# A diffusion backbone's last stretch, turned from features x tokens to tokens x features

## The chip, the cores and the metric

The kernel runs on one core of a Trainium2 chip. A core has TensorE for matmuls (the profile lists its weight loads apart, as PEld), VectorE (DVE), ScalarE (ACT), GpSimd (POOL) and SyncE (SP), which here issues nearly all DMAs. The metric is the time of one execution on the device in microseconds (us), less is better. Times are medians of several runs; the profile is of one execution, taken by the hardware profiler.

## The reference

Two layers work on 256 latent tokens and 256 context tokens of 1024 features. Layer 0 mixes tokens with a convolution module, layer 1 with a bidirectional mLSTM of 4 heads; each is followed by an MLP with a squared ReLU. Shift, scale and gate of every sub-layer (`sh1, sc1, g1, sh2, sc2, g2`) come from a map of a conditioning vector, called adaLN; the latents use `c`, the context `c_ctx`. Only the latents are returned, so in layer 1 the context ends with the mixer's state.

```python
def adaln(cvec, w, b):
    return jnp.split(jax.nn.silu(cvec) @ w + b, 6, axis=-1)

def mlstm_output(feats, h_f, h_b, gn_g, skip, w_down):
    ...
    y = (hn.astype(xc.dtype) + skip * xc) * jax.nn.silu(z)
    return y @ w_down

...
        u = modulate(h, sh1, sc1)
...
        h = layer_norm(ALPHA * h + g1 * y, ln1_g[i], ln1_b[i])
        h = layer_norm(ALPHA * h + g2 * sq_relu_mlp(modulate(h, sh2, sc2), mlp_w1[i], mlp_w2[i]), ln2_g[i], ln2_b[i])
```

## The kernel before

All activations stand as features x tokens: 128 features on the partitions, tokens along the free axis. A matmul therefore takes a 128x128 block of a weight as its stationary operand and lets the tokens move past it: 512 columns where latents and context go together, 256 where only the latents are left, which is the case in the queries, the output gates, `w_down` and the whole last MLP.

Every product is made of three matmuls (`mm3`, lines 175 to 181): the operands are split into a rounded high part and the remainder, and high x high, high x low and low x high are summed in PSUM. Weights arrive by `raw_load` (1 MB, three buffers, line 150) on SP's queue; `split` (lines 154 and 155) makes the high part on ScalarE and the low part on VectorE, four buffers of 128x1024 each, `wh` and `wl`.

The adaLN map is cut into 12 units of 512 outputs for each layer. `Ada` computes a unit on TensorE (line 291). `AdaV` computes it on VectorE: a step loads 128x512 of the weight into the one buffer `ar` (line 353) and adds its product with a scalar column to an accumulator, once for each of the two streams, context and latents (lines 357 and 359). After eight steps, `rows` sums over the partitions with a matmul by ones (line 372), and `end` transposes the result to feature columns. Layer 1's units 0 to 3 run so during layer 0's MLP (`ada_n1`), units 4 to 8 during the mLSTM's projections (`ada_n2`): one step for each half group of the value projection's last 16, for every second one of the queries, and for every second key tile. The last three units, 9 to 11, run on TensorE after the last down projection, as `fill` between the parts of a norm.

Of layer 1's mixer the diff touches the end. `pair` builds the scores of two heads: 16 key tiles, each projected (272 columns) and multiplied with the conv output (512 columns). Then `Z.att` lists what runs beside what: `o` output gates, `W` decay weights, `A` attention with group norm, `D` the down projection of a head; the number is how many steps of the side chain go with one step of the main one. `down(h)` has eight output tiles, each of 12 matmuls, and line 1417 adds gate times product to the residual `hl`.

A layer norm over features on the partitions is `Norm`: `feed` adds up tiles as they come, takes a mean by a matmul after four (line 446), shifts and squares (lines 461, 466 and 467); `finish` sums by matmuls with a column of ones (line 474), computes the statistics, and spreads them over all partitions with one more matmul (line 507); `apply` multiplies and adds (lines 513 and 514). After the last head `finish` runs with the `fill` units between its parts; the affine then makes the MLP's input `u2` (lines 1459 to 1461).

The last MLP runs in four parts of 1024 hidden features. Each part makes its hidden tiles (w1, eight output tiles, relu, square, split) and multiplies them with w2: eight output tiles of 24 matmuls, each added to `hl` by line 924. The norm is fed in part 3; then line 1475 applies gain and bias and line 1476 stores features x tokens. The host transposes the result.

A scheduler orders each engine's instructions: it takes those that are ready by its own model of the times, in program order where several are. An engine works its queue strictly in order. `pin` keeps chosen matmuls in program order.

## Time and profile before

| | us |
|---|---|
| Median of three runs | 1799.55 |
| Lowest and highest | 1798.92, 1805.72 |
| The profiled execution | 1797.44 |
| Its span, first to last instruction | 1795.7 |

| Engine | busy us | share |
|---|---|---|
| TensorE, matmul | 1743.1 | 97% |
| TensorE, weight load | 1513.9 | 84% |
| VectorE | 1111.0 | 62% |
| ScalarE | 762.7 | 42% |
| GpSimd | 8.4 | 0% |

Busy time of a matmul counts from its start to the modelled end of its pipeline, so neighbours overlap; the pace of TensorE is read from the distance of starts. The granted clock is given for a stretch as a share of full speed. A row of the timeline names start, duration, engine, line, operation, out <- in, the shapes and how many neighbours were merged; in brackets stands how long the engine idled before it and what released it. The stage of the heads ends at about 1567 us, the last MLP runs from 1589.6 to 1778.6 us.

### The profile page before, as it was taken

The page shows a single profiled execution, that of the slowest core. Times are in us where ns is not written, and L with a number is a line of the kernel's source. Part 1 is how long each engine was busy: PE and PEld are TensorE (multiplying, and loading weights), DVE is VectorE, ACT ScalarE, POOL GpSimd, SP SyncE. Part 2 cuts the span into 40 slices and gives each one's busy share as a digit, 9 for nine tenths or more (in the row PEclk, how much of TensorE's full clock was granted, in tenths as well). Part 3 has the DMA queues.
Part 4 walks back from the last instruction along what each step waited for, and adds up shares of the span by engine and source line. Part 5 has one row for each costly group of instructions (what it writes and reads, how often), then busy time and mean ns, then how long its engine had stood idle before and what let it go on. Part 6 is the DMA issues. An engine that isn't in the chain of part 4 may idle for free.

```text
span 1795.7 us, 28106 instructions
## 1 busy us (share of the span) xinstructions
PE 1743.1 (97%) x11410; PEld 1513.9 (84%) x11410; DVE 1111.0 (62%) x2071; ACT 762.7 (42%) x1212; POOL 8.4 (0%) x60
## 2 busy tenths in 40 slices
PE   8999999999999999999999999999999999889996
PEld 5564998878789999966779999988999999869996
DVE  6556996565546878741336644533777767876666
ACT  4311763232223555531424323323767744434443
POOL 0000000000000000000000000000000000000000
PEclk9999999999999999999999999999999999989998
DMA  9424416344323275677546533533534355555551
GB/s 354 157 97 147 158 60 228 123 141 140 112 94 118 82 239 162 206 248 269 211 143 236 205 103 131 185 132 118 186 138 178 120 186 192 173 202 187 186 188 48
DMA packets 67251, 295.65 MB, mean 165 GB/s; under 512 B 6771, under 2 KB 22643, under 8 KB 36145
## 3 DMA queue, kind: packets, MB, share of 16 engines
q1 hardware_dynamic: 49456, 279.16, 44.6%
q10 hardware_dynamic: 17664, 14.69, 2.5%
q8 instruction: 90, 1.47, 0.3%
q14 instruction: 41, 0.33, 0.1%
HBM read 278.09 MB, written 15.73 MB: 164 GB/s over the span
## 4 chain that ended last, share of the span: by engine, by line
PE 88%; DVE 5%; ACT 3%; DMA 2%; issue 1%; SPq 0%; ACTq 0%; DVEq 0%
PE mm L177 25%; PE mm L181 25%; PE mm L180 24%; DVE wl L155 2%; DMA raw<-ada_w 1%; PE fl L291 1%; ACT wh L154 1%; PE fl L718 1%; PE cv L787 1%; PE ln L177 1%; PE ln L181 1%; PE ln L180 1%; PE mm L762 1%; PE cv L181 1%; PE cv L180 1%
## 5 line engine op out<-in xcount | busy, mean ns | idle before, releaser
L154 ACT CAST wh<-raw 128x1024 fp32r<-128x1024 f32 x354 | 367.7, 1048 | 611.2 <-PE mm L180 520.7
L155 DVE TENSOR_TENSOR wl<-raw,wh 128x1024 fp32r<-128x1024 f32 x354 | 430.7, 1221 | 303.4 <-ACT wh L154 301.4
L180 PE MATMUL mm<-u,wh 128*128 128x256 f32 (+1 forms) x1400 | 447.5, 320 | 0.0
L177 PE MATMUL mm<-u,wh 128*128 128x256 f32 (+1 forms) x1272 | 398.5, 314 | 7.4 <-ACT u L1459 2.1
L181 PE MATMUL mm<-u,wl 128*128 128x256 f32 (+1 forms) x1272 | 396.6, 313 | 0.5 <-DVE wl L155 0.5
L180 PEld LDWEIGHTS mm<-u,wh 128*128 128x128 f32 x1400 | 268.3, 192 | 18.5 <-DVE mv L522 0.8
L177 PEld LDWEIGHTS mm<-u,wh 128*128 128x128 f32 x1272 | 243.8, 192 | 29.6 <-ACT wh L154 7.4
L181 PEld LDWEIGHTS mm<-u,wl 128*128 128x128 f32 x1272 | 244.2, 192 | 16.4 <-DVE wl L155 2.3
L177 PE MATMUL mm<-hid,wh 128*128 128x256 f32 (+1 forms) x512 | 166.0, 324 | 0.0
L181 PE MATMUL mm<-hid,wl 128*128 128x256 f32 (+1 forms) x512 | 165.3, 323 | 0.0
L180 PE MATMUL mm<-hid,wh 128*128 128x256 f32 (+1 forms) x512 | 165.3, 323 | 0.0
L177 PE MATMUL mm<-xl,wh 128*128 128x256 f32 x512 | 146.4, 286 | 0.9 <-ACT wh L154 0.7
L180 PE MATMUL mm<-xl,wh 128*128 128x256 f32 x512 | 145.2, 284 | 0.6 <-DVE xl L155 0.6
L181 PE MATMUL mm<-xl,wl 128*128 128x256 f32 x512 | 145.1, 284 | 0.2
L359 DVE SCALAR_TENSOR_TENSOR L<-ar,cs,L 128x512 f32<-128x512 f32 x126 | 90.0, 748 | 56.8 <-DMA ar<-ada_w 56.7
L177 PEld LDWEIGHTS mm<-hid,wh 128*128 128x128 f32 x512 | 97.4, 190 | 7.9 <-issue 0.2
L180 PEld LDWEIGHTS mm<-hid,wh 128*128 128x128 f32 x512 | 97.5, 190 | 7.7 <-issue 0.2
L181 PEld LDWEIGHTS mm<-hid,wl 128*128 128x128 f32 x512 | 97.4, 190 | 7.5
L177 PE MATMUL mm<-xm,wh 128*128 128x512 f32 x256 | 102.9, 402 | 0.0
L177 PEld LDWEIGHTS mm<-xl,wh 128*128 128x128 f32 x512 | 97.8, 191 | 3.7 <-issue 1.7
L181 PE MATMUL mm<-xm,wl 128*128 128x512 f32 x256 | 100.3, 392 | 0.0
L180 PEld LDWEIGHTS mm<-xl,wh 128*128 128x128 f32 x512 | 97.9, 191 | 1.7 <-DVE xl L155 0.8
(417 smaller groups left out, 3006.0 us busy)
## 6 DMA issues: line engine op xcount, KB each, us to landing
raw<-w SPq DMA_DIRECT2D x64, 1024.0 KB, 4.9
raw<-wo SPq DMA_DIRECT2D x32, 1024.0 KB, 4.8
raw<-ada_w SPq DMA_DIRECT2D x30, 1024.0 KB, 5.0
ar<-ada_w SPq DMA_DIRECT2D x72, 256.0 KB, 2.8
raw<-wv SPq DMA_DIRECT2D x16, 1024.0 KB, 5.4
raw<-wqT SPq DMA_DIRECT2D x16, 1024.0 KB, 5.5
raw<-wq SPq DMA_DIRECT2D x16, 1024.0 KB, 5.3
raw<-wk SPq DMA_DIRECT2D x16, 1024.0 KB, 4.9
```

The source lines that it names most:

```text
L154: c = nc.scalar.copy(hi, src)
L155: nc.vector.tensor_tensor(lo, src, hi.bitcast(F32), op=ALU.subtract)
L177: a = nc.tensor.matmul(ps, wh, xh, start=start, stop=False)
L180: nc.tensor.matmul(ps, wh, xl, start=False, stop=False)
L181: nc.tensor.matmul(ps, wl, xh, start=False, stop=stop)
L291: a = nc.tensor.matmul(ps[32 * j:32 * j + 32], cs[:, kt, 14 - 2 * v:46 - 2 * v], blocks[kt], start=first and kt < 4, stop=last and kt >= 4 ...
L359: nc.vector.scalar_tensor_tensor(a, w, c, a, op0=ALU.mult, op1=ALU.add)
L718: nc.tensor.matmul(wqs[0][32 * j:32 * j + 32, :], wgp[0][:, kt, :], raw[:, j * 512:(j + 1) * 512], start=kt == 0, stop=kt == ET - 1, tile_ ...
L762: nc.tensor.matmul(xfs[b], fm, A[0:fm.shape[0], t, sl], start=i == 0, stop=i == len(w_) - 1)
L787: return nc.tensor.matmul(o[r:r + 64, :], g_[:, r:r + 64], ps_[b][i], start=i == 0, stop=i == 1, tile_position=(0, r))
```

## The change

From `w_down` on, the latents stand as tokens x features: 128 tokens on the partitions, 1024 features along the free axis. The activations become the stationary operand, the weights move, 512 columns at a time.

- The residual is transposed once, when the layer's input is made, into `R` (16 TensorE transposes, ScalarE copies), in place of `hl`.
- `down` does two halves of 512 features x two token tiles, 12 matmuls each. VectorE multiplies by the gate row `G1`, GpSimd adds to `R` (VectorE in the last head). It yields four times for a head instead of eight, and the pace in `Z.att` beside head 3 doubles. The last head's order is token tile by token tile, and its second half of weights is split into `pw` buffers.
- The norms take their statistics along the free axis (`bn_stats`, an iterated reciprocal root, all on VectorE). `ln1` transposes the normed tile back for w1, which stays as it was: weights stationary, 256 tokens moving.
- w2's products accumulate in four PSUM banks over all 32 depth tiles. The last four depth tiles are done for token tile 0 first, so that its `finish` lies beside token tile 1. Gain and bias are rows; the output is stored as tokens x features.
- `fill` is gone. Units 6 to 9 are computed by `AdaV` for the latents alone. Units 4, 5, 10 and 11, the gates, go through the new `AdaR`, which adds the bias to a row and stores it in DRAM; `rows` loads it back to all partitions. `ada_n2` steps at every key tile. Units 0 to 3 stay as they were.
- The eight `sel` copies become broadcast views of the identity. The host lays `wdown` and `w2_1` out anew and passes six rows (`rows_d`).

```diff
-    att = [['o0', 'G0 W0 W1', 2.4], ['o1', 'A0 W2', 2.6], ['o2', 'A1 W3 D0', 3], ['o3', 'A2', 2], ['D1 D2', 'A3', 1.8], ['D3', '', 0]]
+    att = [['o0', 'G0 W0 W1', 2.4], ['o1', 'A0 W2', 2.6], ['o2', 'A1 W3 D0', 3], ['o3', 'A2', 2], ['D1 D2', 'A3', 3.6], ['D3', '', 0]]
...
+    class AdaR(AdaV):
...
+        def rows(self, n):
+            ps = psum()
+            nc.tensor.matmul(ps[0:32, :], ones[:, 0:32], self.acc[1], start=True, stop=True, tile_position=(0, 0))
+            b = adp.tile([P, 512], F32, tag="ar", name=nm("ar"))[0:1, :]
+            nc.sync.dma_start(b, self.bias)
+            nc.vector.tensor_tensor(b, ps[0:1, :], b, op=ALU.add)
+            nc.sync.dma_start(self.dst, b)
...
-    ada_g2, ada_n1, ada_n2 = Ada(0, 10, 2), AdaVs(1, 0, 4), AdaVs(1, 4, 8 - Z.fill)
+    g_dr = [dp.tile([1, D], F32, name=f"g_dr{i}") for i in range(2)]
+    ada_g2, ada_n1, ada_n2 = Ada(0, 10, 2), AdaVs([AdaV(1, u, 2) for u in (0, 2)]), AdaVs(
+        [AdaV(1, u, 2, (1,)) for u in (6, 8)] +
+        [AdaR(1, u, g_dr[i // 2][:, i % 2 * 512:i % 2 * 512 + 512], rows_d[i // 2:i // 2 + 1, i % 2 * 512:i % 2 * 512 + 512])
+         for i, u in enumerate((4, 5, 10, 11))])
...
-        t = xp.tile([P, T], F32, name=f"hl{f}")
+        t, tr = tmp("E"), psum("ln")
...
+            for tt in range(2):
+                nc.tensor.transpose(tr[:, tt * C + i * P:tt * C + (i + 1) * P],
+                                    t[:, i * C + tt * P:i * C + (tt + 1) * P], ident)
+        nc.scalar.copy(R[:, :, f * P:(f + 2) * P], tr.rearrange("p (t c) -> p t c", t=2))
...
-            if m % 2:
-                ada_n2.step()
+            ada_n2.step()
...
+        def one(hf, t):
+            ps = psum(Z.dpsum)
+            ts = slice(t * P, (t + 1) * P)
+            for kt in range(4):
+                mm3(ps, yy[h][kt][0][:, ts], yy[h][kt][1][:, ts], *ws[hf][kt], kt == 0, kt == 3)
+            e_ = tmp("E")
+            nc.vector.tensor_tensor(e_, ps, G1[:, HF[hf]], op=ALU.mult)
+            (nc.vector if h == H - 1 else nc.gpsimd).tensor_tensor(R[:, t, HF[hf]], R[:, t, HF[hf]], e_, op=ALU.add)
...
-    ln.finish([fill] * Z.fill + [ada_n3.end])
...
+    def ln1(t):
+        ts = slice(t * P, (t + 1) * P)
+        r, q = row_norm(t)
+        for g_ in range(2):
+            nc.vector.tensor_scalar(R[:, t, HF[g_]], R[:, t, HF[g_]], r, q, op0=ALU.mult, op1=ALU.add)
+            tr = psum("ln")
+            for i in range(4):
+                nc.tensor.transpose(tr[:, i * P:(i + 1) * P], R[:, t, g_ * 512 + i * P:g_ * 512 + (i + 1) * P], ident)
+            y = tmp("S")
+            for i in range(4):
+                f, sl = 4 * g_ + i, slice(i * P, (i + 1) * P)
+                nc.scalar.activation(UH[g_][:, i, ts], tr[:, sl], AF.Identity, scale=ca[:, 1, f:f + 1],
+                                     bias=cb[:, 1, f:f + 1])
+                nc.vector.tensor_scalar(y[:, sl], tr[:, sl], ca[:, 1, f:f + 1], cb[:, 1, f:f + 1],
+                                        op0=ALU.mult, op1=ALU.add)
+            nc.vector.tensor_tensor(UL[g_][:, :, ts], y.rearrange("p (i c) -> p i c", i=4),
+                                    UH[g_].bitcast(F32)[:, :, ts], op=ALU.subtract)
...
+    for b_ in (GA, BA):
+        nc.gpsimd.tensor_scalar(b_, b_, ALPHA, None, op0=ALU.mult)
+    for t in range(2):
+        for b_, op in ((GA, ALU.mult), (BA, ALU.add)):
+            nc.gpsimd.tensor_tensor(R[:, t, :], R[:, t, :], b_, op=op)
...
+    def finish(t, acc):
+        for hf in range(2):
+            e_ = tmp("E")
+            nc.vector.tensor_tensor(e_, acc[t][hf], G2[:, HF[hf]], op=ALU.mult)
+            nc.vector.tensor_tensor(R[:, t, HF[hf]], R[:, t, HF[hf]], e_, op=ALU.add)
+        r, q = row_norm(t)
+        for hf in range(2):
+            o_ = tmp("E")
+            nc.scalar.activation(o_, R[:, t, HF[hf]], AF.Identity, scale=r, bias=q)
+            nc.vector.tensor_tensor(o_, o_, GN[:, HF[hf]], op=ALU.mult)
+            nc.vector.tensor_tensor(o_, o_, BN[:, HF[hf]], op=ALU.add)
+            nc.sync.dma_start(out[t * P:(t + 1) * P, HF[hf]], o_)
...
+            def w2_mm(w, kt, t):
+                ts = slice(t * P, (t + 1) * P)
+                for hf in range(2):
+                    mm3(acc[t][hf], hid[kt][0][:, ts], hid[kt][1][:, ts], w[0][:, HF[hf]], w[1][:, HF[hf]],
+                        c == 0 and kt == 0, c == 3 and kt == DT - 1)
...
+                    if c == 3 and k2 > 1:
+                        last.append(w)
+                    else:
+                        for t in range(2):
+                            w2_mm(w, 2 * k2 + i, t)
+            if last:
+                for t in range(2):
+                    for i, w in enumerate(last):
+                        w2_mm(w, 4 + i, t)
+                    finish(t, acc)
```

More of the change, by code (lines that the diff above doesn't have):

```diff
@@ L1281, in hybrid_kernel @@
     qe = open_pool("qe")
-    sel = [qe.tile([NG, P], F32, name=f"sel{i}") for i in range(8)]
-    for d in range(2):
-        for h in range(H):
-            cidx = gcol(d, h)
-            nc.vector.tensor_copy(sel[d * 4 + h], ident[:NG, cidx:cidx + 1].broadcast_to([NG, P]))
+    sel = {d * 4 + h: ident[:NG, gcol(d, h):gcol(d, h) + 1].broadcast_to([NG, P]) for d in range(2) for h in range(H)}
     mask = qe.tile([P, 2, 2, P], F32, name="mask")
@@ L1469, in hybrid_kernel @@
-    ln = Norm(C, [t[:, :C] for t in [qf.tile([P, T], F32, name=f"ln{i}") for i in range(3)]])
-    mlp(w1_1, w2_1, u2, hl, C, [(1, ad(1, 1, "g2"), slice(0, C))], lambda m, s: ln.feed(hl[m]), HD, after1, pre=pre1)
-    ln.finish()
-    for f in range(DT):
-        xn = ln.apply(f)
-        t = tmp("E")[:, :C]
-        nc.scalar.activation(t, xn, AF.Identity, scale=V("ln2_g1", f), bias=V("ln2_b1", f))
-        nc.sync.dma_start(out[f * P:(f + 1) * P, :], t)
+    UH, UL = [[qf.tile([P, 4, C], F32R, name=f"u{n_}{i}") for i in range(2)] for n_ in "hl"]
@@ L1477, in hybrid_kernel @@
+    mlp1()
     close_pool()
```

158 lines of the change are left out of this document (96 added, 62 removed).

## The prediction

> **What bounds the kernel now.** I read the page's head, then the busy time of the engines cut at the borders of the stages that the diff touches, then the timeline of TensorE at those borders.
>
> ```profile
> span 1795.7 us, 28106 instructions
> ...
> PE 88%; DVE 5%; ACT 3%; DMA 2%; issue 1%; SPq 0%; ACTq 0%; DVEq 0%
> ```
>
> ```profile
> 1440.00:1567.00 127.00, 123.27 (x991) 121.10 (x990) 93.65 (x153) 57.06 (x76) 0.00 (x0) 0.99 0.51 178
> 1567.00:1589.60 22.60, 13.59 (x70) 4.77 (x68) 16.91 (x52) 3.58 (x8) 0.00 (x0) 0.74 0.91 345
> 1589.60:1594.90 5.30, 5.30 (x25) 5.30 (x26) 5.30 (x17) 3.38 (x7) 0.00 (x0) 0.50 0.02 8
> 1594.90:1778.60 183.70, 183.00 (x1519) 182.35 (x1518) 119.27 (x182) 84.05 (x132) 0.00 (x0) 1.00 0.45 155
> 1778.60:1795.70 17.10, 3.24 (x11) 1.54 (x10) 9.61 (x28) 5.51 (x10) 0.00 (x0) 0.62 0.18 61
> ```
>
> The columns of the second view are the stretch, its length, busy PE, PEld, DVE, ACT and POOL, granted clock, DMA share and GB/s. TensorE sets the time nearly everywhere: 88% of the chain, 183.0 of 183.7 us in the last MLP. So an edit counts if it changes what TensorE issues, or if it lies in one of two holes: 22.6 us between the last down projection and the last MLP, and 17.1 us behind the last matmul.
>
> **Fewer, wider matmuls.** `down` and the second MLP matmul swap operands. For w2 before: 8 output tiles x 32 depth tiles x 3 passes = 768 matmuls, 256 columns wide. After: 2 token tiles x 2 halves x 32 x 3 = 384 of 512. For w_down 384 become 192. What one costs is the distance of starts in the TensorE timeline (first and last row of a run of 37 narrow ones, then of 22 wide ones):
>
> ```profile
> 734.76 0.28 PE L180 MATMUL mm<-u,wh 128*128 128x256 f32 x1
> ...
> 739.08 0.28 PE L180 MATMUL mm<-u,wh 128*128 128x256 f32 x1
> ```
>
> ```profile
> 419.74 0.39 PE L181 MATMUL mm<-hid,wl 128*128 128x512 f32 x1
> ...
> 424.50 0.39 PE L181 MATMUL mm<-hid,wl 128*128 128x512 f32 x1
> 424.81 1.05 PE L372 MATMUL mm<-L,ones 128*32 128x512 f32 x4
> 425.80 0.50 PE L177 MATMUL mm<-u,wh 128*128 128x512 f32 x1
> ```
>
> 4.32 us over 36 steps is 0.120 us; 4.76 over 21 is 0.2267. Two narrow ones against a wide one save 0.0133 us, and (768 + 384)/2 = 576 pairs go: **-7.7 us**. The work is the same; only a fixed part per matmul is paid half as often. This needs the splits of the weights to keep up: a 128x1024 pair of wh and wl now feeds 12 x 0.2267 = 2.72 us of TensorE instead of 24 x 0.120 = 2.88, and the longer of its two steps is this:
>
> ```profile
> L155 DVE TENSOR_TENSOR wl<-raw,wh 128x1024 fp32r<-128x1024 f32 x354 | 430.7, 1221 | 303.4 <-ACT wh L154 301.4 <-PE mm L372 1.2
> ```
>
> 1.22 of 2.72 us, with the 32 L924 updates gone from VectorE: I count no stall.
>
> The Trainium skill (TensorE: Matmul & The Clock Gate, Back-to-back issue gap) gives the warm distance as columns / 2.4 + 2.5 ns, so 109 and 216 ns. By it the fixed part is small and the 576 pairs would save 1.5 us; the measured 120 and 227 differ from it by 11 ns each, and I go by them.
>
> **The norms' matmuls inside the stages.** `Norm.feed` put its mean (lines 446 and 474) between the matmuls of the last head and of the last MLP part:
>
> ```profile
> 1562.89 0.69 PE L446 MATMUL ln<-x,inv_h 128*128 128x256 f32 x2
> ...
> 1563.79 0.36 PE L177 MATMUL mm<-og,wh 128*128 128x256 f32 x1
> ```
>
> 0.90 us, twice: **-1.8 us**.
>
> **The hole before the last MLP.** The last matmul of `down` and the first of w1:
>
> ```profile
> 1566.98 0.28 PE L181 MATMUL mm<-og,wl 128*128 128x256 f32 x1
> 1567.19 1.06 PE L291 MATMUL fl<-raw,cs 128*32 128x512 f32 x8
> ...
> 1585.60 1.87 PE L299 MATMUL fl<-fold,F 128*128 128x6 f32 x8 [2.43 <-DVE F L331]
> 1589.59 1.01 PE L177 MATMUL mm<-u,wh 128*128 128x256 f32 x3 [2.11 <-ACT u L1459]
> ```
>
> 22.4 us. In it stand the three adaLN units of `fill`, the norm's columns, its broadcast through TensorE and the affine. The units wait for their weights:
>
> ```profile
> PEld fl L291 <- DMA raw<-ada_w: 7.3, 5, 2.2
> ```
>
> All of that goes; late next is VectorE's own chain. Its prices, from its timeline (wide operations, the rounds of `rsqrt` in the convolution's norm) and the affine's rows:
>
> ```profile
> 92.75 0.67 DVE L776 TENSOR_TENSOR F<-mm,Hc 128x512 f32<-128x512 f32 x1
> 93.34 0.68 DVE L777 TENSOR_TENSOR F<-mm,Hs 128x512 f32<-128x512 f32 x1
> ...
> 180.47 0.20 DVE L801 BATCH_NORM_AGGREGATE mv<-bst 128x2 f32<-128x12 f32 x1
> ...
> 183.19 0.27 DVE L524 TENSOR_SCALAR mv<-mv 128x1 f32<-128x1 f32 x1
> 183.50 0.16 DVE L525 SCALAR_TENSOR_TENSOR mv<-mv 128x1 f32<-128x1 f32 x1
> 183.70 0.27 DVE L524 TENSOR_SCALAR mv<-mv 128x1 f32<-128x1 f32 x1
> ...
> 184.62 0.15 DVE L804 SCALAR_TENSOR_TENSOR mv<-mv 128x1 f32<-128x1 f32 x1
> 184.81 1.00 DVE L806 TENSOR_SCALAR u<-u,mv 128x512 f32<-128x512 f32 x2
> ```
>
> ```profile
> 1588.93 4.04 ACT L1459 ACTIVATE u<-hl,cb,ca 128x256 fp32r<-128x256 f32 x8 [12.73 <-DVE cb L409]
> ```
>
> A wide operation takes 0.68 us and the next can start after 0.60; a round of `rsqrt` takes 0.51. The aggregate (0.20 plus about 0.1 to the next), three short steps of 0.2, four rounds and the closing one are then some 3.1 us; the row of before took 4.3 (180.47 to 184.77) with other work put between. Low end for the second token tile, nothing in its way: product, add and statistics 3 x 0.68, norm 3.1, scaling 0.5, four transposes 0.6, four quarter-width affines about 1.0 (half of the 0.5 spacing at L1459 each), difference 0.68: **8 us** until the first four depth tiles stand. High end, VectorE doing in a row what is left of both tiles (two chains 6.2, four scalings 1.6, 16 affines 3.2, differences 2.4, products, adds and statistics 2.4, two splits of w1 that wait for the buffers of the last head 2.3): **18 us**. The first tile's sums are ready 5.4 us before the last matmul and the two chains fill each other's gaps, so I take a little under the middle, 12.5: **-9.9 us**. The other four depth tiles have 48 x 0.12 = 5.8 us more. TensorE was idle long enough before that 25 matmuls came at half clock (third row of the stages, 5.3 us); I leave that as it is.
>
> **The tail.** Last matmul 1778.33 + 0.28; the span ends at 1795.7.
>
> ```profile
> 1778.33 0.28 PE L181 MATMUL mm<-hid,wl 128*128 128x256 f32 x1
> ```
>
> ```profile
> 1787.51 5.89 SPq L1476 DMA_DIRECT2D out<-E  x8
> ```
>
> ```profile
> L740 ACT ACTIVATE E<-mm,vecs 128x512 f32<-128x512 f32 x8 | 5.5, 684 | 3.9 <-PE mm L181 3.8
> ```
>
> After: product, add, statistics 2.0, norm 3.1, ScalarE 0.68, gain and bias 1.4, the second half 1.2, store 0.3 + 2.3 (last issue at 1793.4 to the end): 11 us at best. `finish(0)` starts 24 x 0.2267 = 5.4 us before the last matmul and needs some 9 on VectorE, so it reaches 3.5 us into the tail: 15 at worst. I take 14: **-3.1 us**.
>
> **What TensorE gets in addition.** Eight VectorE units of one stream call `rows` eight times where five units of two streams called it five times. A call blocks TensorE from 424.81 to 425.80; its four records of 0.6 us overlap (two streams in separate column strips), so one stream is between 0.5 and 1.0: I take 1.0, 8 x 1.0 - 5 x 1.0 = **+3.0** (low end -1). The residual is transposed once by 16 transposes:
>
> ```profile
> 861.20 0.60 PE L1071 MATMUL ln<-ident,vt 128*128 128x128 f32 x4
> 861.73 1.07 PE L718 MATMUL fl<-raw,wgq 128*32 128x512 f32 x8
> ```
>
> 0.53 for four: **+2.1**.
>
> **At nothing.** VectorE's adaLN steps become 64 of one update, not 40 of two (48 against 60 us), but their 256 KB loads rise by 24 and reach into the second pair of heads, where there were none:
>
> ```profile
> L359 DVE SCALAR_TENSOR_TENSOR L<-ar,cs,L x126: 742/747/754, 269.3 to 1135.4; 128x512 f32<-128x512 f32 x126
> ...
>   DMA ar<-ada_w: 56.7, 37
> ```
>
> ```profile
> 1000.00:1050.00 50.00, 50.00 (x334) 45.77 (x333) 30.27 (x58) 17.05 (x30) 0.00 (x0) 1.00 0.49 171
> ...
> 1200.00:1250.00 50.00, 50.00 (x306) 43.01 (x305) 15.13 (x42) 14.22 (x27) 0.53 (x1) 1.00 0.36 122
> ```
>
> VectorE waits 56.7 us for these loads in 37 places, and TensorE stays at 50.00 of 50 beside it; the second pair has VectorE at 15 of 50. Without that cover it is the slow rival below. `AdaR.rows` adds a wait: VectorE for the bias row, behind it the splits of the next keys; SP's queue holds the store of the row until that sum, and behind it the next raw load. Four such places, with one raw load for every two key tiles and three buffers ahead: nothing, at worst one such wait for TensorE in each, 4 x 1.5 us (56.7 / 37). The eight `sel` copies go, `D0` to `D2` give VectorE one 0.68 us product where two narrower updates stood, and the shorter `down` chain is paced by 3.6, so the ratio to head 3 stays. TensorE's 3.7 idle us between 1440 and 1567 may shift by 3 either way.
>
> **Sum.** -7.7 - 1.8 - 9.9 - 3.1 + 3.0 + 2.1 = **-17.4 us** on the profiled 1797.44 (its span of 1795.7 and 1.7 around it): 1780.0. The median shown, 1799.55, lies 2.1 above the profiled run, so **1782**. All good ends (hole 8, tail 11, rows -1): -28.9, 1771. All bad ends (hole 18, tail 15, 3 more in the stages): -7.9, 1792.
>
> **Rivals.**
> *No gain by width.* If the fixed part lay in the columns and a wide matmul cost two narrow ones, the 7.7 us fall away: 1790. Against it are the two runs of starts; for it, that they come from other stages. 0.08.
> *GpSimd holds VectorE up.* 12 adds of 128x512 move to it, and six 128x1024 operations in the MLP. The nearest row:
>
> ```profile
> L1289 POOL TENSOR_SCALAR mask<-tri 128x128 f32<-128x128 f32 x1 | 0.3, 340 | 0.1
> ```
>
> Four times that is 1.36 us, 12 of them 16 us. If VectorE stood still meanwhile and TensorE waited as long: 1799.6 - 17.4 + 16 = 1798, no change. Against: VectorE has 33 of 127 us free there. The Trainium skill (SBUF — State Buffer, Who interferes with whom) says the two engines exclude each other when a VectorE operation has two SBUF inputs and GpSimd reads; no row here shows it, since POOL is busy 0.00 in that stage. 0.11.
> *The new norm is as long as the old hole*, the VectorE queue behind the splits: gain without that term, 1792. 0.07.
> *Slower: the adaLN loads reach TensorE.* 24 more loads at the mean wait 56.7 / 37 = 1.53 us are 36.7 us on VectorE; with the bias rows behind them the PSUM buffers of the key projection run out. All on the path: 1799.6 - 17.4 + 36.7 = 1819; it decides from half of that. Against: the same arrangement in the first pair cost TensorE nothing. 0.06.
>
> **Chances.** Forecast 0.68; no gain by width 0.08 is still faster, just; GpSimd and the long norm 0.18 lie within 0.5% (1790.6 to 1808.5, about what a measurement of this kernel can tell from no change); slower 0.06. Faster 0.76, same 0.18, slower 0.06. The range 1771 to 1792 takes in both ends of the sum.
>
> **What would show it.** Starts of w2's matmuls 0.227 apart; 10 to 15 us between the last matmul of `down` and the first of w1; 12 to 15 us behind the last matmul; PE still 50 of 50 between 1000 and 1250. I am wrong if TensorE waits in the key projection, or if that hole stays above 18.

## The result, and the profile after

The changed kernel takes **1811.02 us** (median of 10 runs, 1807.17 to 1814.71), the kernel before beside it 1799.24. The ratio is 1.0066, with a 95% interval of 1.0053 to 1.0080: slower by some 12 us, where 17 us less were forecast. The profiled execution has a span of 1812.1 us (1814.03 with what lies around it).

The first table cuts both spans at the same events: first matmul of `wv`, first matmul of the output gates, last one of the gates, last down projection, start of the steady last MLP, last matmul. The columns are those of the stage table in the prediction. In the changed kernel, "steady" means from the first matmul of a low part (`ul`); four matmuls of high parts stand already in the stretch before. The kernel before:

```profile
0.00:751.50 751.50, 732.56 (x4368) 606.80 (x4369) 498.76 (x993) 302.76 (x496) 7.08 (x55) 1.00 0.44 153
751.50:1250.30 498.80, 497.89 (x2990) 417.76 (x2989) 222.96 (x382) 169.71 (x274) 0.90 (x4) 1.00 0.53 182
1250.30:1513.30 263.00, 256.78 (x2041) 246.02 (x2042) 195.10 (x341) 172.30 (x258) 0.40 (x2) 1.00 0.47 168
1513.30:1567.00 53.70, 50.70 (x397) 49.34 (x395) 43.08 (x82) 21.46 (x30) 0.00 (x0) 0.97 0.46 156
...
1589.60:1778.60 189.00, 188.30 (x1542) 187.65 (x1542) 124.57 (x197) 87.43 (x139) 0.00 (x0) 0.99 0.44 151
```

The changed kernel:

```profile
0.00:762.20 762.20, 739.91 (x4384) 611.31 (x4385) 496.39 (x987) 300.81 (x493) 6.93 (x53) 0.99 0.44 153
762.20:1268.50 506.30, 502.44 (x2983) 417.62 (x2982) 219.15 (x372) 171.26 (x276) 1.06 (x6) 1.00 0.56 188
1268.50:1535.10 266.60, 258.29 (x1993) 245.47 (x1994) 193.59 (x332) 172.88 (x258) 6.35 (x6) 0.99 0.47 167
1535.10:1589.70 54.60, 47.69 (x247) 39.61 (x245) 45.09 (x67) 20.57 (x28) 13.27 (x8) 0.97 0.46 157
1589.70:1612.10 22.40, 5.47 (x22) 4.07 (x20) 20.66 (x56) 6.79 (x16) 13.33 (x6) 0.60 0.49 175
1612.10:1795.00 182.90, 182.16 (x1148) 166.37 (x1148) 104.69 (x142) 81.54 (x124) 2.21 (x1) 0.98 0.46 156
1795.00:1812.10 17.10, 0.02 (x1) 0.00 (x0) 12.12 (x31) 3.04 (x4) 0.00 (x0) 0.62 0.16 61
```

I call these stretches A (to `wv`), B (to the gates), C (the heads), D (head 3's products and projection), the hole, F (the last MLP) and the tail. The last MLP lost 6.1 us, as forecast. The hole (22.6 before, in the prediction's table, 22.4 now, 22.5 by the starts themselves) and the tail (17.1 and 17.1) lost nothing. A, B, C and D, where I had put +5.1 less the 3.5 that the wide `down` and the norm's matmuls save there, grew by 10.7, 7.5, 3.6 and 0.9.

**The hole.** VectorE, then ScalarE, then GpSimd, from the timelines of the changed kernel (start, duration, engine, operation, in brackets the wait ahead and its releaser):

```profile
1600.83 0.76 DVE L1519 TENSOR_SCALAR S<-ln,ca,cb 128x128 f32<-128x128 f32 x2 [0.21 <-ACT uh L1517]
1601.76 0.76 DVE L1519 TENSOR_SCALAR S<-ln,ca,cb 128x128 f32<-128x128 f32 x2 [0.18 <-ACT uh L1517]
...
1603.14 0.69 DVE L1521 TENSOR_TENSOR ul<-S,uh 128x512 fp32r<-128x512 f32 x1
...
1605.14 1.89 DVE L1521 TENSOR_TENSOR ul<-S,uh 128x512 fp32r<-128x512 f32 x1
...
1609.50 2.58 DVE L1521 TENSOR_TENSOR ul<-S,uh 128x512 fp32r<-128x512 f32 x1
```

```profile
1600.33 2.68 ACT L1517 ACTIVATE uh<-ln,cb,ca 128x128 fp32r<-128x128 f32 x6 [0.31 <-DVE S L1519]
```

```profile
1604.14 2.35 POOL L1534 TENSOR_TENSOR res<-res,GA 128x1024 f32<-128x1024 f32 x1
1606.57 2.67 POOL L1534 TENSOR_TENSOR res<-res,BA 128x1024 f32<-128x1024 f32 x1
1609.20 2.34 POOL L1534 TENSOR_TENSOR res<-res,GA 128x1024 f32<-128x1024 f32 x1
1611.62 2.69 POOL L1534 TENSOR_TENSOR res<-res,BA 128x1024 f32<-128x1024 f32 x1
```

Two things are to be seen. ScalarE (line 1517) and VectorE (line 1519) both read the four transposes in one PSUM bank and take turns, each waiting for the other: two VectorE affines start every 0.93 us. And the difference at line 1521 takes 0.69 us while GpSimd is still at line 1531 (one tensor, until 1604.2), but 1.89 and 2.58 us beside the operations of line 1534 (two tensors). TensorE meanwhile:

```profile
1597.56 1.97 PE L1513 MATMUL ln<-ident,res 128*128 128x128 f32 x8 [7.51 <-DVE res L1510]
1603.16 1.12 PE L1513 MATMUL ln<-ident,res 128*128 128x128 f32 x4 [3.64 <-DVE S L1519]
...
1612.14 0.58 PE L179 MATMUL mm<-ul,wh 128*128 128x256 f32 x1 [5.22 <-DVE ul L1521]
```

**The tail**, VectorE's timeline. The second token block's sums (line 1541 on) stand behind the gain and bias of the first (lines 1546 and 1547), and the rounds of `rsqrt` come once more before the end (the last row closes them):

```profile
1796.66 1.40 DVE L1546 TENSOR_TENSOR E<-E,GN 128x512 f32<-128x512 f32 x2 [0.34 <-ACT E L1545]
1797.97 1.28 DVE L1547 TENSOR_TENSOR E<-E,BN 128x512 f32<-128x512 f32 x2
1799.18 0.69 DVE L1541 TENSOR_TENSOR res<-res,E 128x512 f32<-128x512 f32 x1
...
1805.23 0.16 DVE L1503 SCALAR_TENSOR_TENSOR mv<-mv 128x1 f32<-128x1 f32 x1
```

**The residual's transposes** come at the end of `up_z`, in TensorE's timeline:

```profile
668.05 0.67 PE L1042 MATMUL ln<-ident,E 128*128 128x128 f32 x4
...
670.00 0.41 PE L1042 MATMUL ln<-ident,E 128*128 128x128 f32 x2 [0.81 <-DVE E L1039]
...
671.27 0.67 PE L1042 MATMUL ln<-ident,E 128*128 128x128 f32 x4 [0.39 <-DVE E L1039]
```

VectorE's row for it says why TensorE waits: the scaled residual takes one of four E buffers, and these wait for `up_z`'s stores.

```profile
669.45 0.73 DVE L1039 TENSOR_SCALAR E<-x,al 128x256 f32<-128x256 f32 x2 [0.75 <-DMA zs_dr<-E]
```

### The profile page after: what moved, and what is told of

The parts are those of the page before. It is cut to its first block, busy times and chain, and to the rows that moved or that the text cites. A ratio compares the mean times of both kernels' runs of the same rounds, so it can differ in the third digit from the quotient of the medians.

```text
span 1812.1 us, 26781 instructions
## 1 busy us (share of the span) xinstructions
PE 1736.0 (96%) x10770; PEld 1484.5 (82%) x10770; DVE 1091.7 (60%) x1983; ACT 756.9 (42%) x1198; POOL 43.1 (2%) x78
## 4 chain that ended last, share of the span: by engine, by line
PE 82%; DVE 7%; DMA 4%; ACT 4%; issue 2%; SPq 0%; DVEq 0%; ACTq 0%
PE mm L176 22%; PE mm L180 22%; PE mm L179 22%; DMA ar<-ada_w 3%; DVE wl L154 2%; PE ln L176 2%; PE ln L180 1%; PE ln L179 1%; PE cv L180 1%; PE cv L179 1%; PE cv L176 1%; ACT wh L153 1%; PE fl L290 1%; PE cv L806 1%; PE fl L737 1%
## 5 line engine op out<-in xcount | busy, mean ns | idle before, releaser
L179 PE MATMUL mm<-u,wh 128*128 128x256 f32 (+1 forms) x1152 | 377.8, 328 | 0.0
L176 PE MATMUL mm<-u,wh 128*128 128x256 f32 (+1 forms) x1024 | 327.9, 321 | 6.3 <-DVE E L763 2.9
L180 PE MATMUL mm<-u,wl 128*128 128x256 f32 (+1 forms) x1024 | 327.4, 321 | 0.9 <-DVE wl L154 0.9
L179 PEld LDWEIGHTS mm<-u,wh 128*128 128x128 f32 x1152 | 220.5, 191 | 18.3 <-DVE mv L541 0.8
L176 PEld LDWEIGHTS mm<-u,wh 128*128 128x128 f32 x1024 | 196.2, 192 | 28.1 <-issue 8.0
L180 PEld LDWEIGHTS mm<-u,wl 128*128 128x128 f32 x1024 | 196.7, 192 | 16.5 <-DVE wl L154 2.0
L358 DVE SCALAR_TENSOR_TENSOR L<-ar,cs,L 128x512 f32<-128x512 f32 x112 | 81.7, 747 | 85.8 <-DMA ar<-ada_w 85.7
L180 PEld LDWEIGHTS mm<-xl,wl 128*128 128x128 f32 x512 | 99.2, 194 | 1.7 <-DVE wl L154 1.0
L176 PE MATMUL mm<-hid,wh 128*128 128x512 f32 (+1 forms) x256 | 93.4, 365 | 0.0
L179 PE MATMUL mm<-hid,wh 128*128 128x512 f32 (+1 forms) x256 | 92.8, 363 | 0.0
L180 PE MATMUL mm<-hid,wl 128*128 128x512 f32 (+1 forms) x256 | 92.8, 363 | 0.0
L179 PE MATMUL mm<-ul,wh 128*128 128x256 f32 x248 | 71.4, 288 | 5.2 <-DVE ul L1521 5.2
L176 PE MATMUL mm<-qq,wh 128*128 128x272 f32 x256 | 74.4, 291 | 0.0
```

Of the source, the lines that this page charges most:

```text
L176: a = nc.tensor.matmul(ps, wh, xh, start=start, stop=False)
L179: nc.tensor.matmul(ps, wh, xl, start=False, stop=False)
L180: nc.tensor.matmul(ps, wl, xh, start=False, stop=stop)
L358: nc.vector.scalar_tensor_tensor(a, w, c, a, op0=ALU.mult, op1=ALU.add)
```

## The experiments

Each is an edit of the changed kernel unless it says otherwise; a ratio is to the kernel before, run beside it. Stretches are from the profiled run of each, cut as above.

**GpSimd out of the hole.**

```diff
-        nc.gpsimd.tensor_scalar(b_, b_, ALPHA, None, op0=ALU.mult)
+        nc.vector.tensor_scalar(b_, b_, ALPHA, None, op0=ALU.mult)
...
-            nc.gpsimd.tensor_tensor(R[:, t, :], R[:, t, :], b_, op=op)
+            nc.vector.tensor_tensor(R[:, t, :], R[:, t, :], b_, op=op)
```

> The six 128x1024 operations that scale the residual by ALPHA times gain and bias go from GpSimd to VectorE, nothing else. Theory G (GpSimd holds VectorE up): in the changed kernel three of the four differences ul<-S,uh last 1.9, 2.6 and 2.4 us while GpSimd works, 0.69 while it rests; now all four last 0.7 us, the hole between down's last matmul and the steady run of w1 falls from 22.2 to 17 to 18 us, and the time by about 4 us against the changed kernel (1811). Rival B (ScalarE and VectorE take turns on one PSUM bank): the differences get shorter but the affines' turns of 0.93 us stay, and the hole shrinks by under 2 us, since the six operations now queue on VectorE itself.

1812.19 us, ratio 1.0067 (1.0041 to 1.0093); hole 22.7. The four differences all take 0.7 us now, yet nothing is won: the work that blocked VectorE stands in VectorE's own queue, all six operations inside the hole. (The 0.69 of the changed kernel, put down to a resting GpSimd above, fell beside its line 1531.)

**A bank for each reader** (eight transposes instead of four, into two banks).

```diff
-            tr = psum("ln")
-            for i in range(4):
+            tr, tr2 = psum("ln"), psum("cv")
+            for tr_ in (tr, tr2):
+                for i in range(4):
...
-                nc.vector.tensor_scalar(y[:, sl], tr[:, sl], ...
+                nc.vector.tensor_scalar(y[:, sl], tr2[:, sl], ...
```

> The transposes of ln1 are made twice, into one PSUM bank for ScalarE's affines and another for VectorE's; GpSimd stays as it is. Theory B (the two engines take turns on one bank): the pairs of affines, now 0.93 us each in turn, 16 pairs, run side by side at 0.46 or less, a group of four falls from 3.7 to about 2 us, the hole from 22.2 to 15 to 17 us, the time by 5 to 7 us against 1811. Rival G (GpSimd alone is the delay): turns or no turns, the differences wait for GpSimd until it ends, hole at 20 or more, time at 1809 to 1811. Rival: both engines read at the same pace whatever the bank, then the affines' rows don't change.

1803.37 us, ratio 1.0034 (1.0016 to 1.0051); hole 19.6. VectorE's affines start every 0.33 us now, and without the turns the hole is 2.9 us shorter, doubled transposes included. The median falls by more, 7.7 us; in the profiles B is 3.6 us shorter too, where nothing was edited.

**Both.**

> Both edits of the two runs beside it. If the two causes add up, the hole falls from 22.2 to about 12 us, which is what the prediction took, and the time by about 10 us against 1811, to about the time before (1799). If one hides the other, no more than the better of the two alone.

1803.52 us, ratio 1.0021 (1.0008 to 1.0035); hole 17.5. Together they take 5.0 us out of the hole, GpSimd's part (2.1) only once the turns are gone; the median shows no gain over two banks alone.

**Head 3 handed out faster.**

```diff
-['D1 D2', 'A3', 3.6]
+['D1 D2', 'A3', 4.8]
```

> Only the pace of head 3 beside the down projections of heads 1 and 2 goes from 3.6 to 4.8, so that more of the down projection is left to cover the end of head 3. Theory (cover): TensorE's 4.9 us wait for the last head's yy before its first matmul and the half clock behind it go, time 4 to 6 us less than 1811. Rival (VectorE is the bound there: it works without a gap from 1555 to 1605): yy comes no earlier, the wait stays within 1.5 us and the time within 2 us of 1811.

1810.29 us, ratio 1.0059 (1.0037 to 1.0080). D falls from 54.5 to 50.5 and the hole grows from 22.5 to 26.1: the same VectorE work is only waited for at another place. VectorE is busy 48.5 of the 50 us from 1555 to 1605 in the changed kernel.

**The gate units left out.**

```diff
-        [AdaR(1, u, g_dr[i // 2]..., rows_d...) for i, u in enumerate((4, 5, 10, 11))])
+        )
...
-    G1 = rows(..., g_dr[0])
+    G1 = rows(..., rows_d[0:1])
...
-            ada_n2.step()
+            if m % 2:
+                ada_n2.step()
```

> The changed kernel without the four gate units of layer 1 (units 4, 5, 10, 11): their 32 steps, four column sums and row writes are left out, the gate rows are the bias rows alone, and the adaLN step runs at every second key tile as before. Theory (the adaLN units cost on the path, by their column sums and by VectorE standing behind the ar loads): the stretch from the first wv matmul to the first gate matmul, 506.2 us in the changed kernel and 498.8 before, falls by 4 to 7 to 499-502, and the time to 1804-1807. Rival (the adaLN work is hidden, the 7 us are the clock): the stretch stays at 503-506 and the time within 2 us of the changed kernel's 1811.

1804.97 us, ratio 1.0031 (1.0012 to 1.0050). The gates are the bias rows alone here. B is 497.2, 9.0 under the changed kernel's profile and 4.0 to 6.0 under the 501.2 to 503.2 of the eleven other profiled runs that have its code there.

**The adaLN part alone**, in the kernel before. All eight units run on VectorE for the latents alone, the gates too as feature columns, without rows through DRAM.

```diff
-ada_g2, ada_n1, ada_n2 = Ada(0, 10, 2), AdaVs(1, 0, 4), AdaVs(1, 4, 8 - Z.fill)
+ada_g2, ada_n1, ada_n2 = Ada(0, 10, 2), AdaVs([AdaV(1, u, 2) for u in (0, 2)]), AdaVs([AdaV(1, u, 2, (1,)) for u in (4, 6, 8, 10)])
...
-    ln.finish([fill] * Z.fill + [ada_n3.end])
+    ln.finish()
```

> The kernel before with only the adaLN part of the change: units 4 to 11 of layer 1 for the latents alone on VectorE, a step at every key tile, no TensorE units between the sums of the norm ahead of the last MLP. The layout stays features x tokens. Theory (the adaLN part costs 4 to 7 us where it runs): the stretch from wv to the first gate matmul grows from 498.8 to 502-505; the hole ahead of the last MLP shrinks by 0 to 4 since three units leave it; the time is 1800-1805. Rival (the adaLN part is free, all the loss is from the layout): the time is 1795-1799, at or under the kernel before.

**1795.23 us**, ratio 0.9979 (0.9964 to 0.9995): a little faster than the kernel before (some 3 us). Two of its stages, B and the hole:

```profile
749.90:1254.00 504.10, 502.51 (x2990) 418.11 (x2989) 220.17 (x376) 174.42 (x282) 1.06 (x6) 1.00 0.56 191
...
1572.30:1586.60 14.30, 4.32 (x14) 2.45 (x12) 10.64 (x30) 3.51 (x7) 0.00 (x0) 0.64 0.29 107
```

B pays 5.3 us, and the hole falls from 22.6 to 14.3 with the old norm and the old layout. So the gain that I had seen in the new norm was that of the three units that leave the hole, and the new norm gave it back.

**The residual early**: scaled in place in its own tiles, transposed between the matmuls of `up_z`.

```diff
-    for f in range(0, DT, 2):
-        t, tr = tmp("E"), psum("ln")
+    def res():
+        for f in range(0, DT, 2):
+            tr = psum("ln")
+            for i in range(2):
+                t = x[f + i][:, HI]
+                nc.vector.tensor_scalar(t, t, al[:, 0, f + i:f + i + 1], ...
...
+        if i % 2:
+            next(sres, None)
```

> The changed kernel with the residual scaled in place in its own tiles during up_z, and its 16 transposes put between the matmuls of up_z instead of behind the last of them. Theory (the residual costs its place, behind the four E tiles that wait for z's stores): the start of wv, 762.3 us in the changed kernel, comes 2 to 4 us earlier, and the time is 1807-1809. Rival (the cost is the transposes themselves): under 1 us, 1810-1811.

1802.58 us, ratio 1.0017 (0.9997 to 1.0036): 8.4 us under the changed kernel, more than either theory gave. TensorE's windows show where some of it lies. The changed kernel, then this one:

```profile
624.60:627.10 2.50, 0.04 (x2) 0.02 (x1) 2.46 (x6) 2.47 (x6) 0.00 (x0) 1.00 0.09 30
...
628.20:631.70 3.50, 3.50 (x19) 3.50 (x19) 2.23 (x6) 1.58 (x3) 0.00 (x0) 0.51 0.55 162
...
666.00:673.00 7.00, 5.80 (x48) 5.25 (x47) 5.67 (x13) 3.38 (x6) 0.00 (x0) 1.00 0.53 199
```

```profile
616.00:640.00 24.00, 22.66 (x182) 21.57 (x181) 21.90 (x45) 20.90 (x37) 0.00 (x0) 1.00 0.61 174
660.00:673.00 13.00, 13.00 (x111) 13.00 (x110) 7.23 (x10) 6.03 (x8) 0.00 (x0) 1.00 0.72 238
```

In the changed kernel the first `up_z` matmuls wait 2.46 us (1.02 here, 1.38 before), right behind that wait 3.5 us run at half clock, and 1.2 us of the stretch of the transposes stand idle. Here the clock stays full and the transposes leave no gap. From the last w2 matmul of the layer before to the first `wv` matmul it is 142.2 us in the kernel before, 148.4 to 151.1 in the nine profiled runs with the late residual, and 143.7 to 145.1 in the six with the early one. The means of the two groups lie 6.0 us apart; the rest of the 8.4 is not explained.

**One reader for the bank**, and the residual's gain and bias on VectorE inside the last MLP.

```diff
-                nc.scalar.activation(UH[g_][:, i, ts], tr[:, sl], AF.Identity, ...
...
+            nc.scalar.copy(UH[g_][:, :, ts], y.rearrange("p (i c) -> p i c", i=4))
             nc.vector.tensor_tensor(UL[g_][:, :, ts], ...
...
-            nc.gpsimd.tensor_tensor(R[:, t, :], R[:, t, :], b_, op=op)
+            nc.vector.tensor_tensor(R[:, t, :], R[:, t, :], b_, op=op)
...
+            if c in (1, 2):
+                affine_r(c - 1)
```

> The changed kernel with a norm in which VectorE alone reads the PSUM bank of the transposes, ScalarE makes one 512 wide copy of VectorE's product, and the residual's gain and bias run on VectorE during the last MLP instead of on GpSimd beside the norm. Theory (the hole is the two engines' turns on one bank and GpSimd's pass beside VectorE): the hole, 22.5 us in the changed kernel and 17.5 with both causes taken out at the price of doubled transposes, is 15 to 17.5; the time is 1803-1806. Rival (VectorE is full from head 3's product on, so that the hole follows VectorE's work whoever reads which bank): the hole stays at 19 or more.

1804.78 us, ratio 1.0028 (1.0013 to 1.0043); hole 17.6, just past the theory's range and under the rival's 19. VectorE's affines now run without a gap, six in 2.00 us:

```profile
1594.43 2.00 DVE L1517 TENSOR_SCALAR S<-ln,ca,cb 128x128 f32<-128x128 f32 x6
1596.55 0.69 DVE L1520 TENSOR_TENSOR ul<-S,uh 128x512 fp32r<-128x512 f32 x1
```

**The additions of heads 0 to 2 on VectorE.**

```diff
-            (nc.vector if h == H - 1 else nc.gpsimd).tensor_tensor(R[:, t, HF[hf]], ...
+            nc.vector.tensor_tensor(R[:, t, HF[hf]], ...
```

> The changed kernel with the 12 additions of heads 0 to 2 to the residual on VectorE instead of GpSimd. Theory (GpSimd's additions stand in VectorE's way beside the other work of the heads, as its gain and bias do in the hole): the stretch of the heads (first to last gate matmul) falls from 266.6 by 1 to 3, D stays, the time is 1808-1810. Rival (the stretch is longer because the splits of a whole half of w_down come at once, and 12 more VectorE operations of 0.69 us make it no better): 266-268 and 1811-1813.

1813.11 us, ratio 1.0075 (1.0048 to 1.0103); C 268.2, D 53.2, hole 24.5. Moving the additions wins nothing: C is 266.6 to 269.1 in the runs that leave them on GpSimd and the heads in order, and what D loses (1.3) the hole more than gains (2.0). They do hold VectorE up, though. In D of the changed kernel these rows stand:

```profile
1559.22 1.32 POOL L1452 TENSOR_TENSOR res<-res,E 128x512 f32<-128x512 f32 x1 [4.99 <-DVE E L1451]
1559.33 2.29 DVE L154 TENSOR_TENSOR wl<-raw,wh 128x1024 fp32r<-128x1024 f32 x1
...
1566.64 1.21 DVE L154 TENSOR_TENSOR wl<-raw,wh 128x1024 fp32r<-128x1024 f32 x1
1566.80 2.17 POOL L1452 TENSOR_TENSOR res<-res,E 128x512 f32<-128x512 f32 x1 [2.10 <-DVE E L1451]
```

A split of VectorE that starts just behind a GpSimd addition takes 2.29 us (a second one 1.98), the 86 others from the heads to the hole 1.2. A GpSimd addition that starts just behind a split takes 2.17 (four of the twelve take 2.2), the others 1.3 to 1.4: the later of the two waits. On VectorE the 12 additions cost 0.69 us each, which eats the gain.

**Residual, norm, square root and tail together.** ScalarE's square root and one reciprocal replace the rounds; the gain and bias of both blocks come behind the sums of both.

```diff
-        rsqrt(r, mv[:, 1:2], q)
+        nc.scalar.activation(q, mv[:, 1:2], AF.Sqrt, bias=eps)
+        nc.vector.reciprocal(r, q)
...
-                    finish(t, acc)
+                    rq.append(finish(t, acc))
+                for t in range(2):
+                    outs(t, *rq[t])
```

> The changed kernel with the early residual and the one-reader norm of the two last runs together, ScalarE's square root and one reciprocal in place of VectorE's four rounds in the row norms, and the last gain and bias of token block 0 put behind the sums of block 1. If the causes add up: -8.4 for the residual, -6.2 for the norm, -3 to -4 for two chains of some 2 us in the hole, -4 for one chain and 2.6 us of order in the tail, so 1788-1792 with a hole of 13-15 and a tail of 12-13.5. Rival (they share one bound, VectorE from head 3's product to the last MLP, and a chain through ScalarE waits as long as the rounds): hole 17 or more, tail 15 or more, 1795-1798.

**1786.97 us**, ratio 0.9925 (0.9903 to 0.9948), a little under the theory's range. Hole, F and tail:

```profile
1577.00:1590.70 13.70, 5.63 (x23) 4.09 (x22) 13.41 (x36) 2.44 (x5) 0.00 (x0) 0.59 0.70 269
1590.70:1771.90 181.20, 180.50 (x1149) 164.72 (x1148) 107.74 (x142) 83.73 (x128) 0.00 (x0) 0.99 0.46 157
1771.90:1783.70 11.80, 0.02 (x1) 0.00 (x0) 8.42 (x17) 2.05 (x4) 0.00 (x0) 0.59 0.24 89
```

**More buffers for the adaLN weights.**

```diff
-            w = adp.tile([P, 512], F32, tag="ar", name=nm("ar"))
+            w = tmp("S") if self.streams == (1,) and self.i % 3 else adp.tile([P, 512], F32, tag="ar", name=nm("ar"))
```

> The changed kernel with two more buffers for the adaLN weights from wv on (they are free there), nothing else. Theory (VectorE's queue stands behind an adaLN load that can't be issued before the last step gave its one buffer back): VectorE's waits for the adaLN loads between 1000 and 1260 fall to less than half, the stretch from wv to the first gate matmul falls from 506.2 to 500-503, the time to 1806-1809. Rival (the column sums on TensorE and its waits behind VectorE cost the time, not the loads): 503.5 or more, within 2 us of 1811.

1809.5 us, ratio 1.0055 (1.0039 to 1.0070). VectorE's waits for these loads between 1000 and 1260 fall from 35.7 us to 10.5, and B in the profile is 501.8, as the theory had it; but the median is only 1.5 us under the changed kernel's, less than these runs can tell, and eleven other runs with one buffer show 501.2 to 503.2. So VectorE stands behind the loads, and TensorE hardly notices.

**All of it, and the splits of `w_down` in four steps.**

```diff
+            w2_ = []
+            for i in range(2):
+                w2_.append(split_w(raw[:, i * 1024:(i + 1) * 1024]))
+                yield
```

> All of it together: early residual, one-reader norm, ScalarE's square root, the tail's order, three adaLN buffers, and the splits of w_down of one head given out in four steps instead of two. If each step pays by itself: 2 to 5 under the run with residual, norm, root and tail, so 1784-1789, with 500-503 from wv to the first gate matmul and 263-266 for the heads. Rival (the steps of w_down shift head 3's chain and the wait ahead of its product grows): D over 57 and no gain over that run.

1791.05 us, ratio 0.9954 (0.9935 to 0.9973): 4 us over the run without the buffers and the spread splits. C is 269.1 (a stall of 3.3 us ahead of head 3's weights), hole 16.9. The theory's gain did not come; nor did the rival's D of over 57: it is 55.1.

**Head 0's projection ahead of head 3's weights**, in the run of 1786.97.

```diff
-['o2', 'A1 W3 D0', 3]
+['o2', 'A1 D0 W3', 3]
```

> The run with early residual, one-reader norm, square root and tail order (1786.97), with head 0's down projection handed out ahead of head 3's decay weights instead of behind them. Theory (four splits of w_down come together where the decay weights of head 3 need the same two engines, and the clock halves behind the stalls): the 3.2 us of stalls 188 to 192 us into the heads go, the half-clock stretch behind them too, the heads fall from 266.9 to 263-265, the time to 1782-1785. Rival (the splits stall TensorE wherever they come): stalls of the same size at another place, 266-268, within 1.5 us of 1787.

**1783.57 us**, ratio 0.9907 (0.9886 to 0.9928), the lowest median here, though its interval overlaps that of the run that it edits. C is 264.0, from 266.9. In the run that it edits, TensorE's timeline has these rows at the end of `o2`:

```profile
1443.21 0.45 PE L1332 MATMUL cv<-pw,dsel 128*36 128x256 f32 x3 [0.93 <-DVE pw L154]
1444.86 0.39 PE L176 MATMUL mm<-xl,wh 128*128 128x256 f32 x1 [1.20 <-ACT wh L153]
1446.12 0.39 PE L180 MATMUL mm<-xl,wl 128*128 128x256 f32 x1 [0.75 <-DVE wl L154]
```

With three smaller ones ahead of them the stalls there are 4.2 us. Here stalls of 1.57 and 0.76 us stand at the projection itself, and 0.21 and 0.34 at head 3's weights: 2.9 in all, and 3.4 us at half clock follow in both runs. Another 1.2 us of the 2.9 that C loses lie at a wait early in the heads (2.06 us, 0.87 here), which the edit does not touch. So the time is the theory's, but the stalls moved much as the rival had it.

**Head 3 faster, once more**, now in the run of 1786.97, and then with head 0's projection moved as well.

> The run with early residual, one-reader norm, square root and tail order (1786.97), with head 3's steps handed out faster (4.8 for 3.6) beside heads 1 and 2. In the changed kernel the same edit moved 4 us of stall from head 3's product into the hole behind it. Theory (VectorE is no longer full there): the wait ahead of head 3's product, 5.4 us, falls to 3, the hole stays at 13.7-15 and the time is 1783-1786. Rival (VectorE is still the bound of that stretch): D falls by 3 and the hole grows by 2 or more, 1786-1788.

> The two edits of the other runs of this call together: head 0's down projection ahead of head 3's weights, and head 3's steps at 4.8. If they add up: 1779-1783; if either gives its stall to the other place: 1784-1788.

1786.59 us, ratio 0.9933 (0.9909 to 0.9957): D falls by 5.6 to 50.5 and the hole grows by 4.7 to 18.4. Both edits: 1787.0 us, ratio 0.9921 (0.9894 to 0.9948), with D 49.9, C 263.9, hole 18.4. VectorE is still the bound of D and hole together (busy 48.1 us of 50.5 from 1540 to 1590.5 in the first), so pace is worth nothing there. Moving head 0's projection lowers C again, by 4.4 from the 268.3 of the first run, but not the median. So that it shortens C is shown twice; that it shortens the kernel is seen in one pair of runs and not in the other.

## Why the prediction was wrong, step by step

**Fewer, wider matmuls, and the norm's matmuls: right.** F should lose 5.1 and 0.9 us, and lost 6.1 (four matmuls, 0.5 us, went into the hole, and F has 0.5 us more at half clock). The last rows of w2 in TensorE's timeline start 0.227 us apart:

```profile
1794.17 0.39 PE L176 MATMUL cv<-wh,hid 128*128 128x512 f32 x1
1794.40 0.39 PE L179 MATMUL cv<-wl,hid 128*128 128x512 f32 x1
1794.63 0.39 PE L180 MATMUL cv<-wh,hid 128*128 128x512 f32 x1
```

The smaller gain of `w_down` can't be read by itself in C and D, where stalls changed at the same time.

**The hole before the last MLP: the step that failed first.** I took 12.5 with 18 as the worst; it was 22.4. VectorE is busy 20.66 of the 22.4 us, so the picture of the high end was right, VectorE doing in a row what is left of both tiles, and a value under the middle was not. Two of its prices were wrong. Everything up to the first affine took 10.2 us (1589.65 to 1599.90) against 12.5 in that sum, as the two chains did fill each other's gaps: two rounds start every 0.56 us, one every 0.51. The affines and differences then took 12.2 us (to 1612.14) against 5.6, and one of each even came later. "16 affines 3.2" is 0.2 us each (the low end has 0.25); VectorE alone starts one every 0.33, and in turns with ScalarE two every 0.93. The differences, put at 0.6 each, took this:

```profile
L1521 DVE TENSOR_TENSOR ul<-S,uh 128x512 fp32r<-128x512 f32 x4 | 7.6, 1898 | 0.1
```

Three of them, 5.2 us, lie in the hole. The six GpSimd operations that hold them up I had named, but I priced only the 12 additions of the heads. The two excesses, 6.6 us, less the 2.3 of the first part are the 4.4 between 18 and 22.4. Two banks took 2.9 off the hole, both edits 5.0. With one reader and GpSimd's work moved it is still 17.6, the bad end of my range. Only with the rounds gone too is it 13.7, and those I had priced rightly. So 12.5 belonged to a norm that the change did not have.

The turns have a rule in the Trainium skill (PSUM — Partial Sum Buffer, PSUM bank collisions raise a hardware error): the compiler's scheduler makes instructions of two engines on one bank and the same partitions depend on each other, two reads included. The waits between lines 1517 and 1519 agree. GpSimd's hold is the rule that the prediction cited from the Trainium skill (SBUF — State Buffer, Who interferes with whom): 0.69 against 1.89 and 2.58 us for an operation with two SBUF inputs agrees with it, and the affines of line 1519, which read PSUM, keep their 0.4 us beside the same GpSimd work. The 0.69 us beside line 1531, which reads SBUF too, don't fit it, as far as GpSimd's recorded spans can be trusted. Nor is line 1531 harmless: two scalings of line 1510 that start at 1598.25 beside it took 1.72 us, where two at 1596.96 took 0.99.

**What the old hole was made of.** With the adaLN part alone the old norm's hole is 14.3 us, not 22.6. I put the whole fall down to the new norm and did not ask what the old norm would take without the three units; the best form of the new one, 13.7, is hardly shorter. So the condition of the rival that the new norm would be as long as the old hole came true, at 0.07, though more by the bank and GpSimd than by the splits, and its 1792 did not, as other terms failed too.

**The tail: too small, past its bound.** 14 taken, 15 at worst, 17.1 measured. That `finish(0)` reaches into the tail was seen; that its gain and bias would stand ahead of the second block's sums, 1796.66 to 1799.18, was not. With the order turned and the rounds gone it is 11.8, against the 11 that I gave as the best; no run parts the two.

**The residual's transposes: the price was right, the place was not counted.** 2.1 us were put for TensorE. But the eight scalings that the kernel before ran in VectorE's gaps wait for E buffers now, and the transposes for them; with the longer first wait of `up_z` and its half clock that is 6.2 to 8.9 us over the 142.2 of before. With the early residual 1.5 to 2.9 are left, around the 2.1.

**Eight calls of `rows`: about right.** +3.0 was put; B grew by 2.4 to 4.4 in eleven runs with the same code. The changed kernel's own profile has 7.5: it has three stalls, of 1.91, 1.09 and 0.68 us, of which only the second waits for an adaLN step. From 1000 to 1250 its TensorE is busy 248.2 us of 250, where the kernel before has 249.2, so the sign that I had named, TensorE waiting in the key projection, hardly showed.

**At nothing: half wrong.** The adaLN loads, my slow rival at 1819, are not it: more buffers gave 1.5 us, not told from zero. But the order around the heads was not free. In C, +3.6: head 0's projection splits two 128x1024 pieces of `w_down` at once where it split one before, beside head 3's weights. Moving it took 2.9 and 4.4 out of C, of which 1.3 and 1.2 are stalls at that place. That it is the bundling isn't shown: the run that spreads the splits, with other edits, has a C of 269.1. In D, TensorE waits 4.89 us ahead of head 3's product, where it waited 2.31 before:

```profile
1577.21 0.80 PE L176 MATMUL mm<-wh,og 128*128 128x512 f32 x1 [4.89 <-ACT og L153]
```

That wait is no loss by itself: three runs with the faster pace shortened it and got it back in the hole.

**The size of it all.** The changed kernel came out 29.0 us over the forecast. By place, its profile, which lies 3 us over the median, is over it by 9.7 in the hole, 3.1 in the tail, 8.6 in A, 4.5 in B and 8.0 in C and D together. Put right in the five places (residual, reader, rounds, tail, order of the heads), the same layout takes 1783.57. That this comes near the 1782 forecast does not make the steps right, and is luck: the gain needed edits that the change did not have, and part of it is the adaLN part's, which gives 1795.23 in the old layout.

Of A's 10.7, 4.4 lie ahead of the last w2 matmul of layer 0, which comes at 606.9 to 616.0 us in the 17 profiled runs. Most of that spread is the run and not the edit (last section). A smaller part is the change's: a stall of TensorE near 52 us lasts 2.85 to 2.88 us in all 15 runs of the new layout, 2.10 and 2.09 in the two of the old. Why stays open.

## What to carry to other kernels

When a wait ends, price what is late next by the engine that does it, and count on that engine everything that shares its bank or its port, not only its own instructions: two readers of one PSUM bank take turns, and work on GpSimd is not free while VectorE is the bound. Before crediting a gain to the new form, ask what the old form would take with the same work removed; one run of that half alone would have shown it. A piece of work that is moved needs buffers where it lands: the 16 transposes were cheap, their place behind another stage's stores was not.

## What the runs showed of the hardware

**A stall of TensorE can cost more than its own length.** The first wait of `up_z` is 2.46 us in all nine profiled runs with the late residual, and 3.4 us at about half clock follow in all nine. It is 1.02 to 1.44 us in the eight others, and in none of them does the clock fall there.

**Such stretches differ between runs in code that no edit touches.** Of the 15 runs that stall for 2.85 us near 52 us, two show no half clock from there to the last w2 matmul of layer 0. Over all 17 profiled runs that matmul comes at 606.9 to 607.7 us where the clock was never halved before it (three runs), at 608.2 to 611.0 with 6.8 us at half clock (ten), at 613.5 and 613.8 with 13.7 (two, the changed kernel among them), and at 615.5 and 616.0 with 20.5 (two). From 62 to 200 us, first in the last run (both edits), then in the run with head 0's edit alone, which is the same kernel up to the heads:

```profile
62.00:200.00 138.00, 134.32 (x600) 79.77 (x600) 72.13 (x172) 35.66 (x57) 0.00 (x0) 0.95 0.37 136
```

```profile
62.00:200.00 138.00, 134.60 (x655) 85.18 (x654) 79.44 (x189) 38.53 (x65) 0.00 (x0) 0.99 0.39 143
```

The granted clock is 0.95 and 0.99, and the first `wv` matmul comes at 759.9 and 752.1. So single profiles of this kernel differ by several us before the part under study begins, and stretches were compared rather than spans.

**VectorE and GpSimd hold each other up, the later one waiting.** Beside an operation of the other with two SBUF inputs, a VectorE split took 2.29 us where 1.22 is usual, and a GpSimd addition 2.17 where 1.29 is.
